# One projection of the second half computed before the attention instead of in between

## The chip, the cores and the metric

The kernel runs on one core of one Trainium2 chip. The metric is device time in microseconds (us) of one execution. TensorE (PE) does matrix products, VectorE (DVE), ScalarE (ACT) and GpSimd (POOL) do elementwise work, and SyncE (SP) issues nearly all DMAs, in the order of its own queue. Every engine takes its instructions in a fixed order and waits on semaphores.

## The reference, cut to what matters

A single decoder layer with 2048 tokens and a model width of 1024, all in float32:

```python
h = rmsnorm(x, g_norm)
proj = h @ w_in                       # 2048 x 1024 times 1024 x 9216
a_u, a_v, a_gate, q, k, v, b_gate, gate_logits = split(proj)
y_a = spatial_gating(gelu(a_u), gelu(a_v)) * silu(a_gate)
y_b = dilated_attention(q, k, v) * silu(b_gate)     # 16 heads, 3 patterns of keys
g_a, g_b = split(sigmoid(gate_logits))
merged = g_a * (y_a @ w_proj_a) + g_b * (y_b @ w_proj_b)
out = rmsnorm(x + merged @ w_out, g_final)
```

The change is about `b_gate`: columns 6144 to 7167 of `w_in`, called bg here, for the second half of the tokens (1024 of 2048). It is needed only where an attention output is multiplied by it.

## The kernel before, in words

**Precision.** Each float32 product is made of three products of split operands (hi times hi, hi times lo, lo times hi; `mm3`, L103). One output block of 128 channels by 512 tokens takes 8 slices of the inner dimension, so 24 matmuls of 128 by 512. The kernel's unit of work for bg is 16 such blocks per half (8 blocks of channels, 2 quarters of 512 tokens).

**Two ways to compute a projection.** `unit_T` computes the blocks one by one, 24 matmuls each, so 16 x 24 = 384 for bg of one half. It loads 128 columns of weights at a time (tile `wraw`), and GpSimd splits them into `whi` (L85) and `wlo` (L86). `unit_S` computes a 2 by 2 arrangement of blocks with seven block products in place of eight (Strassen's scheme in Winograd's form). It works with sums of weight blocks, which VectorE makes (L346 to L350), and sums of activation blocks (tiles `T`), which are made once per half. Each product has 12 matmuls, four groups of seven products make the same 16 blocks, so 336 matmuls. The price is more work elsewhere: ScalarE and GpSimd split the weights per product (L83, L86, tile `wc`), and VectorE adds the products together (L363).

**Stages.** For each half of the tokens: normalisation, v, the a_v projection, then k, q, and branch A (a_u and a_gate), nearly all with `unit_S`. In the first half two more `unit_S` follow: bg and the first gate (`ga`). In the second half the program goes from branch A to the attention after `restore`, which brings four activation tiles back (L150, L151, L144, L145) that had held sums. The results go to DRAM, bg to `bg_d`, from where the attention's last step loads them (L741).

**Attention and fill.** The function `window` writes out 16 heads, each with three patterns in the order p = 2, 1, 0, each with four groups g = 0 to 3. A group is in three stages: S (scores on PE, L639 and L640; bias, scale and row maximum on VectorE, L647; exponential on ScalarE, L653), T (transposes, L669; a split into `ph` on ScalarE, L672, and `pl` on VectorE, L673) and O (output products, L686 to L688; copy on ScalarE, L689). The stages are written in a software pipeline: S of group j, T of group j-2, O of group j-3. For each head come, in pieces between the stages, `combine` of the head before (VectorE L708 to L732, GpSimd L729, on every second head transposes L739 and L743) and `permuted`, which reorders Q, KH and KL (L600, L598) for the coming pattern.

Into this stream go the other products, the *fill*: block products of `unit_T`, cut into runs of 8 matmuls (`every` = 8). A run is put in when the fill counted so far lags behind the attention counted so far times a ratio. This ratio is the total fill, 5.2 us per block, less 8 blocks, over a nominal cost of the attention. Six blocks (144 matmuls) come before the first group, and what is left comes at the end. The stage `final` (the projection of the attention and the output) follows.

In this text heads are numbered 0 to 15, and "group p2 g0" means the stretch from the first output product (L686) of that group to the first of the next group. In this stretch PE does the O stage of this group, the S stage of the group three later, the T stage of the group one later, and whatever fill stands between.

## Time and profile before

| | |
|---|---|
| median of 3 runs (lowest to highest) | 2685.8 us (2683.05 to 2686.45) |
| the profiled execution: its time, its span | 2690.79 us, 2688.8 us |
| mean granted TensorE clock | 0.974 |
| busy: PE, DVE, ACT, POOL | 93%, 67%, 47%, 33% |
| attention's window (first fill matmul to the last output copy) | 1326.3 to 2281.4 us |
| of this, from the first output copy on | 1380.7 to 2281.4 us |

Where a row of the profile has the form `L103 PE MATMUL pj<-X,whi ... x1284 | 440.5, 416 | ...` it gives the line, engine, operation, tiles written and read, the number of instructions, their busy time in us and the mean duration of one in ns, and then the idle time before them. A row of stretches has begin and end, the length, and the busy time and number of instructions per engine, then the granted PE clock and the share and rate of the DMA engines. A PE that counts as busy isn't always at its peak, since the duration of a matmul reaches into the next one: in a dense stretch one of 128 by 512 starts every 0.23 us and lasts 0.39 us.

### The profile page before, as it was taken

Reading aid. Unit: us, or ns where it says so; the run is one execution under the profiler, and the core shown is the slowest. Engines: PE = TensorE matmul, PEld = TensorE weight load, DVE = VectorE, ACT = ScalarE, POOL = GpSimd, SP = SyncE. Lnnn points to the kernel's source line nnn. Section 1 sums busy time; section 2 is a strip of 40 time slices with the busy share of each in tenths; the row PEclk is TensorE's granted clock in tenths of the full one; section 3 lists DMA queues with packets and bytes.
Section 4 is the critical chain, followed back from the end, with each engine's and each line's share of the span. In section 5 each row is a group of like instructions: output and inputs, shape, how many; then the busy total and the mean of one; then the engine's idle time right before and its main releaser. Section 6 shows DMA issues by size and latency. Waiting matters only on the chain.

```text
span 2688.8 us, 45128 instructions
## 1 busy us (share of the span) xinstructions
PE 2503.2 (93%) x16736; PEld 2122.7 (79%) x16736; DVE 1794.8 (67%) x3633; ACT 1255.1 (47%) x2481; POOL 888.2 (33%) x633
## 2 busy tenths in 40 slices
PE   5969999999998999999899899989889898899998
PEld 5969888888887898888677778878777777677787
DVE  5864767756258547677457877787989888545533
ACT  4335333343333353333257777676767665222221
POOL 0325554444444444544222222333333333000000
PEclk9989999999999999999899999999999999999999
DMA  7744333253453343323356646677777876755541
GB/s 232 162 126 142 102 118 106 94 171 116 153 167 89 87 138 115 122 95 114 99 142 158 185 127 181 177 195 201 200 217 194 237 206 176 239 168 184 169 132 63
DMA packets 463995, 410.00 MB, mean 152 GB/s; under 512 B 150432, under 2 KB 384288, under 8 KB 463776
## 3 DMA queue, kind: packets, MB, share of 16 engines
q1 hardware_dynamic: 463344, 407.05, 51.7%
q8 instruction: 132, 2.16, 0.3%
q14 instruction: 87, 0.71, 0.1%
q10 hardware_dynamic: 432, 0.07, 0.0%
HBM read 297.35 MB, written 109.71 MB: 151 GB/s over the span
## 4 chain that ended last, share of the span: by engine, by line
PE 67%; DVE 13%; DMA 10%; issue 4%; ACT 3%; POOL 1%; SPq 0%; ACTq 0%; DVEq 0%; POOLq 0%
PE pj L103 32%; PE pt L103 15%; PE ss L103 10%; PE pt L669 3%; DVE S L647 2%; PE ss L639 2%; DVE pl L673 1%; DVE X L145 1%; PE ss L640 1%; DMA v_d<-vst 1%; DMA wraw<-in_w_in 1%; DMA OC<-o_d 1%; DMA o_d<-ob 1%; PE pt L512 1%; DVE OC L727 1%
## 5 line engine op out<-in xcount | busy, mean ns | idle before, releaser
L103 PE MATMUL pj<-X,whi 128*128 128x512 f32 x1792 | 602.3, 411 | 16.5 <-POOL whi L85 11.1
L86 POOL TENSOR_TENSOR wc<-wraw,wc 128x512 fp32r<-128x512 f32 x240 | 327.4, 1372 | 318.7 <-ACT wc L83 307.2
L103 PEld LDWEIGHTS pj<-X,whi 128*128 128x128 f32 x1792 | 342.5, 195 | 88.1 <-POOL whi L85 12.0
L103 PE MATMUL pj<-X,wlo 128*128 128x512 f32 x896 | 369.2, 412 | 7.6 <-DVE wlo L86 4.0
L647 DVE CUSTOM_DVE_ANT_0 S<-ss,B,niqk 128x256 f32<-128x256 f32 (+1 forms) x768 | 284.3, 418 | 22.0 <-PE ss L640 21.8
L673 DVE SCALAR_TENSOR_TENSOR pl<-pt,ph 128x512 f16<-128x512 f32 x320 | 204.8, 653 | 93.3 <-ACT ph L672 92.0
L653 ACT ACTIVATE S<-S,ob 128x128 f32<-128x128 f32 (+1 forms) x512 | 193.4, 437 | 72.5 <-DVE ob L647 71.5
L83 ACT CAST wc<-wraw 128x512 fp32r<-128x512 f32 x240 | 145.2, 618 | 165.3 <-PE pt L103 78.8
L85 POOL TENSOR_SCALAR whi<-wraw 128x1024 fp32r<-128x1024 f32 x64 | 69.9, 1093 | 442.9 <-PE pj L103 393.2
L103 PEld LDWEIGHTS pj<-X,wlo 128*128 128x128 f32 x896 | 175.1, 195 | 46.5 <-DVE wlo L86 6.9
L672 ACT ACTIVATE ph<-pt 128x512 f16<-128x512 f32 x320 | 177.2, 565 | 61.1 <-PE pt L669 37.0
L103 PE MATMUL ss<-T,wc 128*128 128x512 f32 x768 | 188.2, 394 | 0.0
L103 PE MATMUL pt<-X,wc 128*128 128x512 f32 x768 | 185.2, 390 | 0.0
L103 PE MATMUL pj<-WO,X 128*128 128x512 f32 x768 | 180.7, 395 | 4.1 <-ACT X L872 3.9
L103 PEld LDWEIGHTS pj<-WO,X 128*128 128x128 f32 x768 | 144.2, 188 | 40.0 <-ACT X L872 5.2
L669 PE MATMUL pt<-ident,S 128*128 128x128 f32 x1200 | 168.6, 278 | 3.4 <-DVE pl L673 3.3
L86 POOL TENSOR_TENSOR wcl<-wraw,wch 128x1024 fp32r<-128x1024 f32 x52 | 129.2, 2486 | 121.4 <-ACT wch L83 97.2
L103 PEld LDWEIGHTS ss<-T,wc 128*128 128x128 f32 x768 | 143.6, 188 | 32.0
L103 PEld LDWEIGHTS pt<-X,wc 128*128 128x128 f32 x768 | 143.9, 188 | 30.3
L86 POOL TENSOR_TENSOR wlo<-wraw,whi 128x1024 fp32r<-128x1024 f32 x64 | 164.5, 2571 | 5.3
L103 PE MATMUL pt<-T,wc 128*128 128x512 f32 x672 | 165.0, 394 | 0.0
L669 PEld LDWEIGHTS pt<-ident,S 128*128 128x128 f32 x1200 | 141.7, 144 | 15.1 <-DVE pl L673 4.4
(229 smaller groups left out, 5777.8 us busy)
## 6 DMA issues: line engine op xcount, KB each, us to landing
wraw<-in_w_in SPq DMA_DIRECT2D x64, 1024.0 KB, 5.7
V<-v_d SPq DMA_DIRECT2D x48, 520.0 KB, 4.8
o_d<-ob SPq DMA_DIRECT2D x32, 528.0 KB, 5.1
OC<-o_d SPq DMA_DIRECT2D x32, 528.0 KB, 4.7
wraw<-in_w_in SPq DMA_DIRECT2D x32, 512.0 KB, 5.4
wraw<-in_w_proj_a SPq DMA_DIRECT2D x32, 512.0 KB, 5.3
wraw<-in_w_proj_b SPq DMA_DIRECT2D x32, 512.0 KB, 4.7
xt<-in_xT SPq DMA_DIRECT2D x60, 256.0 KB, 4.3
```

The lines of the kernel that those rows point to most:

```text
L83: nc.scalar.copy(hi, raw)
L85: nc.gpsimd.tensor_scalar(out=hi, in0=raw, scalar1=1.0, scalar2=0.0, op0=ALU.mult, op1=ALU.add)
L86: self.w_lo.tensor_tensor(out=lo, in0=raw, in1=hi.bitcast(F32), op=ALU.subtract)
L103: self.pe = nc.tensor.matmul(out, st(a, k), mv(b, k), start=first and n == 0, stop=last and n == len(todo) - 1)
L145: self.x_lo.tensor_tensor(out=X[k][1], in0=src, in1=X[k][0].bitcast(F32), op=ALU.subtract)
L512: nc.tensor.matmul(px[:, i * P:(i + 1) * P], av[:, 4 * q + i], w, start=True, stop=True)
L639: nc.tensor.matmul(ps[:, i, :n], q, KH[:, w], start=True, stop=False)
L647: nc.vector.tensor_tensor_reduce(out=S[:, j, :n], in0=ps[:, i, :n], in1=B[:, bo:bo + n], scale=self.niqk[:, pr:pr + 1], scalar=3e38, op0=A ...
L653: nc.scalar.activation(S[:, i, :rng[i]], S[:, i, :rng[i]], AF.Exp, bias=ob[:, i, 65:66], scale=-1.0)
L669: self.pe = nc.tensor.transpose(px[:, j * P:(j + 1) * P], G["S"][:, i, c * P:(c + 1) * P], self.ident)
L672: nc.scalar.activation(ph[:, :n], px[:, :n], AF.Copy, scale=PSCALE)
L673: nc.vector.scalar_tensor_tensor(out=pl[:, :n], in0=px[:, :n], scalar=PSCALE, in1=ph[:, :n], op0=ALU.mult, op1=ALU.subtract)
```

## The change: what it does

bg of the second half is computed by `unit_S` right after branch A and ahead of `restore`, so before the attention. It no longer stands in the fill, whose total is given as 64 blocks instead of 80.

```diff
@@ Prog.run
                     drain(branch_a)
+                if hf == 1:
+                    drain(self.unit_S(X, win, 6144, self.ev_bg, qds))
                 if hf == 0:
                     drain(self.unit_S(X, win, 6144, self.ev_bg, qds))
                     drain(self.unit_S(X, win, 7168, self.ev_gate(self.ga_d), qds))
@@ fill()
             e = self.every
-            yield from self.unit_T(X, win, 6144, self.ev_bg, (2, 3), every=e)
             yield from self.unit_T(X, win, 7168, self.ev_gate(self.ga_d), (2, 3), every=e)
@@ 
-            self.window(at, fill(), 80 * 5.2)
+            self.window(at, fill(), 64 * 5.2)
```

How this moves instructions is seen on PE. First, the end of branch A. The last row that stays is a product of branch A (`wc` is a weight piece of `unit_S`); X and T are activations and their sums, `ss` a bank of PSUM.

```order
 L103 MATMUL pt<-T_3_1_6995,wc 128x512
 L103 MATMUL pt<-T_3_0_6994,wc 128x512
+L103 MATMUL ss<-X_0_0_6521,wc 128x512
+L103 MATMUL ss<-X_0_1_6522,wc 128x512
+L103 MATMUL ss<-X_0_0_6521,wc 128x512
+L103 MATMUL ss<-X_1_0_6523,wc 128x512
+L103 MATMUL ss<-X_1_1_6524,wc 128x512
```

In all 336 rows of this kind are new here, the 28 products of the unit; behind them the first row of the fill comes as before.

Second, PE in the attention, head 4, group p2 g0, from the last score product of the S stage on (`KLP` is the reordered low part of the keys). Before:

```order
L640 MATMUL ss<-KLP,Q 128x256
L103 MATMUL pj<-X_2_0_6525,wlo 128x512
L103 MATMUL pj<-X_3_0_6527,whi 128x512
L103 MATMUL pj<-X_3_1_6528,whi 128x512
L103 MATMUL pj<-X_3_0_6527,wlo 128x512
L103 MATMUL pj<-X_4_0_6529,whi 128x512
L103 MATMUL pj<-X_4_1_6530,whi 128x512
L103 MATMUL pj<-X_4_0_6529,wlo 128x512
L103 MATMUL pj<-X_5_0_6531,whi 128x512
L669 MATMUL pt<-ident,S 128x128 x4
L686 LDWEIGHTS ph
L686 MATMUL po<-V,ph 128x65
```

With the change, at the same place:

```order
L640 LDWEIGHTS Q
L640 MATMUL ss<-KLP,Q 128x256
L669 MATMUL pt<-ident,S 128x128 x4
L686 LDWEIGHTS ph
L686 MATMUL po<-V,ph 128x65
```

The one run of eight fill matmuls that this group had is gone, and the transposes follow the scores at once.

Third, PE in head 4, group p1 g2, from the last output product of the O stage on (`cb` is the combined output of two heads, whose transposes stand here). Before:

```order
L688 MATMUL po<-V,pl 128x65
L103 MATMUL pj<-X_2_0_6525,wlo 128x512
L103 MATMUL pj<-X_3_0_6527,whi 128x512
L103 MATMUL pj<-X_3_1_6528,whi 128x512
L103 MATMUL pj<-X_3_0_6527,wlo 128x512
L103 MATMUL pj<-X_4_0_6529,whi 128x512
L103 MATMUL pj<-X_4_1_6530,whi 128x512
L103 MATMUL pj<-X_4_0_6529,wlo 128x512
L103 MATMUL pj<-X_5_0_6531,whi 128x512
L739 MATMUL pt<-ident,cb 128x128 x4
L639 LDWEIGHTS Q
L639 MATMUL ss<-KH,Q 128x256
```

With the change:

```order
L688 MATMUL po<-V,pl 128x65
L739 MATMUL pt<-ident,cb 128x128 x4
L639 LDWEIGHTS Q
L639 MATMUL ss<-KH,Q 128x256
L640 LDWEIGHTS Q
```

Here one run of two is gone; the other, between the scores and the transposes, stays. Counted over all 192 groups in this way, 48 runs (384 matmuls) leave:

| group | from 2 runs to 1 | from 1 to 0 | from 0 to 1 |
|---|---|---|---|
| p2 g0 | | 15 | |
| p2 g1 to p1 g1 | 6 | 3 | 5 |
| p1 g2 and p1 g3 | 18 | | |
| p0 g0 to p0 g3 | 3 | 9 | 1 |

A head has 13 or 14 runs before (head 15 has 11) and 10 or 11 with the change (8). The six blocks ahead of the first group, the end of the fill, and the order of the attention's own work stay as they are.

## The prediction

> **What bounds the kernel now.** I read the busy shares first, then the stretches between the stages, then the attention group by group.
>
> ```profile
> PE 2503.2 (93%) x16736; PEld 2122.7 (79%) x16736; DVE 1794.8 (67%) x3633; ACT 1255.1 (47%) x2481; POOL 888.2 (33%) x633
> 560.13:637.27 77.14, 77.14 (x337) 63.07 (x336) 47.50 (x63) 35.38 (x63) 39.25 (x31) 1.00 0.53 174
> 1316.73:1326.31 9.58, 0.00 (x0) 0.00 (x0) 4.99 (x8) 1.43 (x3) 1.05 (x1) 0.62 0.83 238
> 1326.31:1380.70 54.39, 48.82 (x232) 38.10 (x232) 19.12 (x46) 20.68 (x28) 17.64 (x11) 0.91 0.65 174
> 1380.70:2281.40 900.70, 825.25 (x8080) 694.33 (x8080) 744.18 (x2228) 629.48 (x1389) 275.98 (x190) 0.97 0.68 187
> ```
>
> The line of the whole page says PE, 93% busy. But the average hides what matters here. The first stretch is bg of the first half, the very unit that the change writes a second time: PE is busy in all of it. The second is the idle time of PE between branch A and the first fill matmul, the third the six blocks of fill ahead, the fourth the attention. In the fourth PE idles 900.70 - 825.25 = 75 us, and VectorE is busy for 744 of 901 us (83%).
>
> Where is the idle time? Within a head there are two kinds of stretch. First the six groups from p2 g0 to p1 g1, for heads 1 to 14, each row from the first output product of the one to that of the other (14 rows and their sum):
>
> ```profile
> 1426.67:1456.26 29.59, 25.16 (x225) 21.09 (x223) 27.44 (x73) 22.46 (x47) 8.02 (x7) 0.94 0.45 126
> 1482.84:1511.28 28.44, 25.91 (x237) 21.54 (x234) 27.41 (x72) 22.27 (x47) 7.27 (x7) 1.00 0.51 146
> 1537.92:1567.97 30.05, 25.28 (x224) 21.25 (x222) 27.36 (x72) 22.81 (x48) 8.75 (x7) 0.89 0.40 115
> ...
> 2117.87:2148.22 30.35, 24.30 (x224) 19.59 (x224) 26.93 (x81) 21.63 (x45) 11.72 (x10) 1.00 0.84 227
> 2173.35:2202.89 29.54, 24.39 (x227) 20.31 (x227) 29.15 (x79) 20.24 (x43) 11.34 (x9) 1.00 0.53 145
> sum 417.48, PE 356.70 PEld 295.02 DVE 394.60 ACT 307.93 POOL 147.28; mean PE 25.48 PEld 21.07 DVE 28.19 ACT 21.99 POOL 10.52
> ```
>
> Here VectorE is busy for 394.60 of 417.48 us (95%) and PE idles 60.8. VectorE carries the combine of the head before and the reordering of the keys on top of the groups' own work. Then the six groups from p1 g2 to p0 g3:
>
> ```profile
> 1456.26:1482.84 26.58, 25.61 (x280) 21.85 (x278) 17.97 (x71) 18.41 (x43) 3.46 (x2) 1.00 0.67 168
> ...
> 2202.89:2232.00 29.11, 28.89 (x300) 24.60 (x298) 21.87 (x75) 17.30 (x46) 6.90 (x4) 1.00 0.83 252
> sum 387.85, PE 379.54 PEld 323.50 DVE 274.45 ACT 256.45 POOL 104.14; mean PE 27.11 PEld 23.11 DVE 19.60 ACT 18.32 POOL 7.44
> ```
>
> Here it is PE, 98% busy, with VectorE at 71%. So half of a head is bound by VectorE and half by PE, and a fill matmul taken away pays in the second half alone. The waits in the attention's window (total us, times, longest) say the same:
>
> ```profile
> PE ss L639 <- DVE ob L647: 38.7, 59, 4.3
> PE po L688 <- DVE pl L673: 18.4, 17, 3.0
> DVE S L647 <- PE ss L640: 21.8, 21, 4.6
> ```
>
> 57 us of PE's idle time are waits for VectorE, while VectorE waits for scores for 22 us.
>
> **What is added.** 28 products of 12 matmuls, with their weight splits, additions, tanh and 16 stores. The unit of the first half took 77.14 us, and PE was busy without a break while VectorE (47.50), ScalarE (35.38) and GpSimd (39.25) had room. The one of the second half has the same neighbours on one side (the order shows its first product right behind branch A's last); on the other it ends at `restore`, as branch A does now. Its weight loads replace loads of equal size in the fill, and SP has room for them. So I take +77.1 us, at 77.14 / 336 = 0.230 us per matmul. Since the unit was never held up, I see no reason for a range of more than a microsecond on this term.
>
> Does the start of the attention change? Its chain is this:
>
> ```profile
> 1319.56 0.75 DVE L151 SCALAR_TENSOR_TENSOR xt<-xt,gn,rsbc 128x512 f32<-128x512 f32 x1 [0.48 <-DMA xt<-in_xT]
> 1320.37 0.38 SPq L91 DMA_DIRECT2D wraw<-in_w_in  x1
> 1325.21 1.05 POOL L85 TENSOR_SCALAR whi<-wraw 128x1024 fp32r<-128x1024 f32 x1 [30.25 <-DMA wraw<-in_w_in]
> 1326.31 0.80 PE L103 MATMUL pj<-X,whi 128*128 128x512 f32 x1 [9.58 <-POOL whi L85]
> ```
>
> The first fill weights are loaded into memory that `restore`'s last multiplication (its `rsbc`) still holds, and PE waits 9.58 us. With the change `restore` stands behind bg, the same chain follows bg's last product, and in SP's order that load now comes just behind bg's last store instead of just ahead of branch A's. The evacuation has one VectorE operation less (0.69 us) per block. I take 0, between -1 and +1.
>
> **What is taken away.** 48 runs of eight fill matmuls, 384 matmuls, at most 384 x 0.230 = 88.2 us. By the table of the change 29 of them (net) leave the stretch bound by PE and 19 the one bound by VectorE.
>
> *From two runs to one, in the stretch bound by PE: 21.* The profile holds the experiment: p1 g2 and p1 g3 occur with two runs (17 times) and with one (11 times); these are the first row and the sum of each.
>
> ```profile
> 1456.26:1462.36 6.10, 6.10 (x54) 4.94 (x51) 4.15 (x12) 3.99 (x10) 0.00 (x0) 1.00 0.13 46
> sum 110.09, PE 109.20 PEld 90.29 DVE 72.33 ACT 66.89 POOL 13.75; mean PE 6.42 PEld 5.31 DVE 4.25 ACT 3.93 POOL 0.81
> 1511.28:1515.88 4.60, 4.60 (x49) 4.11 (x49) 2.92 (x11) 3.21 (x9) 0.74 (x1) 1.00 0.28 86
> sum 49.05, PE 48.82 PEld 42.23 DVE 40.66 ACT 33.32 POOL 23.41; mean PE 4.44 PEld 3.84 DVE 3.70 ACT 3.03 POOL 2.13
> ```
>
> 110.09 / 17 - 49.05 / 11 = 6.48 - 4.46 = 2.02 us per run. So -42.4 us; the lower bound is the bare matmuls, 21 x 1.84 = 38.6.
>
> *From one run to none, in the same stretch: 8 net, most in p0 g0.* In heads 1 to 14 no group there ran without fill. With one run:
>
> ```profile
> sum 45.98, PE 44.58 PEld 38.30 DVE 33.17 ACT 32.90 POOL 20.29; mean PE 4.05 PEld 3.48 DVE 3.02 ACT 2.99 POOL 1.84
> ```
>
> 11 of p0 g0, 4.18 us each, of which VectorE works 3.02 and ScalarE 2.99. Without the run PE needs 4.18 - 1.84 = 2.34, and VectorE becomes the bound at 3.02: 1.16 us are won, or up to 1.84 where the neighbours, in which VectorE has room, absorb it. I take the middle, 1.5: -12 us, between -9.3 and -14.7.
>
> *In the stretch bound by VectorE: 19 net, 15 of them the only run of p2 g0.* The sum of the 14 stretches of p2 g0, and ScalarE's reordering of Q, which stands in it:
>
> ```profile
> sum 63.65, PE 51.44 PEld 42.09 DVE 60.11 ACT 62.19 POOL 14.45; mean PE 3.67 PEld 3.01 DVE 4.29 ACT 4.44 POOL 1.03
> L600 ACT COPY QP<-Q x15: 4114/4162/4247, 1376.2 to 2171.2; 128x2048 f16<-128x2048 f16 x15
> ```
>
> ScalarE is busy for 62.19 of 63.65 us and VectorE for 60.11, so the 15 runs can win about 0.1 us each there, 1.5 in all. For the other four I take 1 us each, which makes -5.5 us. The bounds are 0 and all the time in which VectorE isn't busy in the six groups: (417.48 - 394.60) / 14 = 1.63 us per head, 26 us for 16.
>
> *bg's evacuation leaves the attention.*
>
> ```profile
> L544 DVE SCALAR_TENSOR_TENSOR tbg<-tbg,pj 128x512 f32<-128x512 f32 x16 | 11.0, 685 | 28.7 <-ACT tbg L543 23.8 <-DMA KH<-k_d 4.9
> L732 DVE TENSOR_TENSOR cb<-OC 128x256 f32<-128x256 f32 x64 | 43.0, 672 | 4.7 <-POOL OC L729 4.7
> L732 DVE TENSOR_TENSOR cb<-OC x60: 405/416/2623, 1436.0 to 2254.4; 128x256 f32<-128x256 f32 x60
> ```
>
> Sixteen of 0.685 us, ten of them among the groups, 6.9 us of VectorE; about half fall into the stretch it bounds: -3.5 us, between 0 and -6.9. The gate's evacuation (ScalarE alone) takes the places, so nothing new waits.
>
> The last two rows bear on a smaller thing. An L732 takes 0.416 us mostly, 0.672 in the mean. By the Trainium skill, page "GPSIMD Engine Reference", section "Specifications", GpSimd shares its memory interface with VectorE, and operations with two inputs from there are held up. The trace agrees in kind (405 to 2623 ns for one shape). By that rule eight weight splits fewer would win some 2 us more; I leave it out.
>
> The sum against the profiled execution (2690.8 us): +77.1 - 42.4 - 12 - 5.5 - 3.5 = **+13.7 us**, 2704.5. The median of the runs lies 5 us lower, and the change should read +13.7 there too: 2685.8 + 13.7, rounded to **2700 us**. With the bounds of the terms it is +30 (77.1 - 38.6 - 9.3 - 0 - 0 = 29.2, and 1 of the start) down to -13 (77.1 - 42.4 - 14.7 - 26 - 6.9).
>
> **The rivals.**
>
> *The slack of VectorE is used.* If PE's runs in the VectorE-bound groups cost time because PE comes late with scores, VectorE's 1.63 us per head would be won: 77.1 - 42.4 - 14.7 - 26 - 3.5 = -9.5, so 2676 us. For it: VectorE's 22 us of waits for scores. Against it: it is 95% busy, and in p2 g0 both VectorE and ScalarE are full. Half of that slack would be near no change.
>
> *The clock.* A p2 g0 without fill leaves PE idle longer: now (63.65 - 51.44) / 14 = 0.9 us, then 2.7. If PE gets half its clock for one more piece of 3.4 us per head, and half of it counts, 1.7 x 16 = 27 us are lost: +41, 2727 us. For it: the granted clock is under 1 in many of these stretches (0.94, 0.89). Against it: of the rows shown, those at 1.00 took 28.44, 29.54 and 30.35 us, and the one at 0.89 took 30.05, so VectorE hides it. It decides where PE's work at half clock outlasts VectorE's 28.2 us. The Trainium skill, page "TensorE: Matmul & The Clock Gate", section "Part 1", gives the piece as about 3.4 us, and says that one idle window throttles the array; the granted clock here agrees with pieces of that order, and no run here shows the threshold.
>
> *The start of the attention gets shorter.* If the first fill weights come while bg's last products run, the 9.58 us go, and the change is about +4: no change. Against it: the order above and `rsbc`.
>
> *The change doesn't shorten the attention at all*, since its own latency sets the pace: +77. Against it stand the 2.02 us per run, so I give it nothing of its own.
>
> **How the numbers follow.** Forecast 0.65, VectorE's slack used 0.13, the clock 0.14, the shorter start 0.08. Under 0.2% (5.4 us) this kernel's measurement doesn't tell a change. The forecast's own range is +3 to +28 (2689 to 2714), of which some 0.12 lie within 5.4 us. So faster 0.12 (nearly all of the slack's rival), the same 0.20 (0.12, and 0.08 of the shorter start), slower 0.68. The range from 2682 to 2722 reaches into the cases on both sides.
>
> **What would show it.** Right: the new unit shows some 77 us with PE busy throughout; p1 g2 to p0 g3 falls from 27.7 us (387.85 / 14) to about 24, with PE still over 95%; p2 g0 to p1 g1 stays at 29 to 30 us, with VectorE at 95% or more and PE's idle time grown from 4.3 us to over 5. Wrong: if p2 g0 to p1 g1 is shorter by over 1.5 us, runs paid there too; if it is longer than 31 us at a granted clock of 0.85, the clock decided; if the idle time ahead of the first fill matmul isn't 9 to 10 us, the start changed.

## The result and the profile after

| | before | with the change |
|---|---|---|
| median (lowest to highest, 4 runs each) | 2686.1 us (2683.1 to 2686.9) | 2716.3 us (2715.3 to 2717.5) |
| ratio, 95% interval | | 1.0115 (1.0097 to 1.0132) |
| span of the profiled execution | 2688.8 us | 2715.1 us |

The changed kernel is 30 us slower; +14 was forecast. Here are its stretches, in the columns of the rows in the prediction: the new unit (from its first matmul to the end of its last), PE's idle time ahead of the first fill matmul, the six blocks of fill ahead, the attention's groups, and the rest.

```profile
1311.97:1389.28 77.31, 77.31 (x337) 62.88 (x335) 41.08 (x59) 26.59 (x44) 28.07 (x21) 1.00 0.23 82
1389.28:1403.33 14.05, 0.00 (x1) 0.00 (x1) 3.88 (x6) 1.43 (x3) 1.05 (x1) 0.66 0.90 218
1403.33:1455.86 52.53, 45.89 (x224) 35.89 (x225) 15.81 (x47) 20.28 (x28) 18.97 (x11) 0.93 0.60 165
1455.86:2312.45 856.59, 750.76 (x7704) 634.02 (x7703) 734.56 (x2212) 617.05 (x1372) 251.52 (x174) 0.94 0.68 187
2312.45:2715.10 402.65, 380.21 (x1608) 302.38 (x1608) 187.02 (x278) 98.78 (x162) 15.87 (x22) 0.98 0.50 160
```

The last stretch of the kernel before was

```profile
2281.40:2688.80 407.40, 381.61 (x1608) 303.82 (x1608) 186.84 (x278) 98.73 (x162) 15.87 (x22) 0.98 0.50 158
```

So by stages: branch A ended at 1311.97 us instead of 1316.73 (-4.8); the new unit took **+77.3**; PE's idle time behind it grew from 9.58 to 14.05 us, **+4.5**; the fill ahead -1.9; the groups 900.70 became 856.59, **-44.1**; the rest -4.8, about as much as the profiled execution of before lay above its own median.

The first of these is scatter: nothing changed before the unit, and over all profiled executions of this document branch A's end lies at 1308.6 to 1316.7 us without the unit (8 executions) and at 1311.3 to 1318.3 with it (12). The idle time is not: it is 9.6 to 10.5 us in the 8 and 12.6 to 14.1 in the 12. PE waits there for the first fill weights (L91, `wraw`), and their load takes longer from issue to landing, last figure in the row, first before and then with the change:

```profile
wraw<-in_w_in SPq DMA_DIRECT2D x1, 512.0 KB, 4.6
wraw<-in_w_in SPq DMA_DIRECT2D x1, 512.0 KB, 9.4
```

So the added unit itself cost what was forecast, and the start of the attention 3.3 us in the mean of these executions, where nothing was expected. The groups should have given back 63.4 us and gave 44.1 in the profiled executions. (By the medians it is 77.3 + 3.3 - 30.2 = 50.4 us for all that follows, so 13 to 19 us are missing there.)

Where are these missing us? The forecast took a head as two stretches. Their sums over heads 1 to 14 with the change, p2 g0 to p1 g1 and p1 g2 to p0 g3, are

```profile
sum 415.79, PE 334.00 PEld 276.52 DVE 387.01 ACT 305.20 POOL 145.88; mean PE 23.86 PEld 19.75 DVE 27.64 ACT 21.80 POOL 10.42
sum 350.99, PE 335.50 PEld 288.49 DVE 277.64 ACT 248.31 POOL 88.17; mean PE 23.96 PEld 20.61 DVE 19.83 ACT 17.74 POOL 6.30
```

against 417.48 and 387.85 before. But this cut hides something: p0 g3, which belonged to the stretch bound by PE, has changed sides. So from here on a head is cut one group earlier. "The head's start" is p0 g3 to p1 g1 (seven groups), "the rest of the head" p1 g2 to p0 g2 (five). The sums over 14 heads, start and rest, before:

```profile
sum 468.15, PE 406.40 PEld 338.11 DVE 433.82 ACT 355.45 POOL 170.72; mean PE 29.03 PEld 24.15 DVE 30.99 ACT 25.39 POOL 12.19
sum 337.23, PE 329.89 PEld 280.59 DVE 235.50 ACT 209.74 POOL 80.70; mean PE 23.56 PEld 20.04 DVE 16.82 ACT 14.98 POOL 5.76
```

and with the change:

```profile
sum 476.83, PE 388.09 PEld 321.66 DVE 443.79 ACT 355.46 POOL 163.02; mean PE 27.72 PEld 22.98 DVE 31.70 ACT 25.39 POOL 11.64
sum 290.50, PE 281.74 PEld 243.64 DVE 221.35 ACT 198.05 POOL 71.44; mean PE 20.12 PEld 17.40 DVE 15.81 ACT 14.15 POOL 5.10
```

In these 14 heads 208 fill matmuls left the rest and 128 the start. The rest won 46.7 us, or 0.225 us per matmul: its full price. The start won nothing. It became **8.7 us longer** with 128 matmuls (28.8 us at the same price) less in it. These are sums over one execution each; a second execution of the same attention, in `e1_no_bg` below, has a start 4.1 us longer than before:

```profile
sum 472.28, PE 382.65 PEld 318.53 DVE 441.11 ACT 354.19 POOL 164.56; mean PE 27.33 PEld 22.75 DVE 31.51 ACT 25.30 POOL 11.75
```

VectorE is busy for 93% of it in both kernels, and its work there grew by 10.0 us, where 3.5 less had been expected.

PE's waits in the attention's window with the change (total us, times, longest):

```profile
PE po L686 <- ACT ob L689: 37.0, 14, 3.3
PE ss L639 <- DVE ob L647: 30.3, 41, 4.6
```

The first row was, before:

```profile
PE po L686 <- ACT ob L689: 11.3, 12, 1.4
```

Once per head PE now waits 2.6 us for ScalarE's copy of an output (L689), which stands behind the 4.2 us copy that reorders Q. The granted clock of the groups fell from 0.97 to 0.94. So there were several suspects: half clock after idle time, ScalarE's copy of Q, VectorE's load, and the place of the lost run itself.

### The profile page after: what moved, and what is told of

Its sections match the earlier page's. It is cut to its first block, busy times and chain, and to the rows that moved or that the text cites. A ratio compares the mean times of both kernels' runs of the same rounds, so it can differ in the third digit from the quotient of the medians.

```text
span 2715.1 us, 45188 instructions
## 1 busy us (share of the span) xinstructions
PE 2500.5 (92%) x16688; PEld 2120.7 (78%) x16688; DVE 1834.8 (68%) x3677; ACT 1270.2 (47%) x2513; POOL 901.2 (33%) x645
## 4 chain that ended last, share of the span: by engine, by line
PE 66%; DVE 14%; DMA 10%; issue 4%; ACT 4%; POOL 1%; SPq 1%; DVEq 0%; POOLq 0%; ACTq 0%
PE pj L103 31%; PE pt L103 16%; PE ss L103 11%; PE pt L669 2%; DVE S L647 2%; DVE pl L673 2%; PE ss L639 1%; DMA v_d<-vst 1%; DMA wraw<-in_w_in 1%; ACT S L653 1%; PE ss L640 1%; DVE X L145 1%; DMA wrow<-in_w_in 1%; PE pt L512 1%; DMA xl<-ya_d 1%
## 5 line engine op out<-in xcount | busy, mean ns | idle before, releaser
L103 PE MATMUL pj<-X,whi 128*128 128x512 f32 x1536 | 523.0, 417 | 20.9 <-POOL whi L85 14.8
L86 POOL TENSOR_TENSOR wc<-wraw,wc 128x512 fp32r<-128x512 f32 x264 | 358.9, 1367 | 358.1 <-ACT wc L83 339.9
L103 PEld LDWEIGHTS pj<-X,whi 128*128 128x128 f32 x1536 | 299.0, 198 | 85.1 <-POOL whi L85 15.7
L103 PE MATMUL pj<-X,wlo 128*128 128x512 f32 x768 | 318.5, 415 | 6.2 <-DVE wlo L86 3.3
L647 DVE CUSTOM_DVE_ANT_0 S<-ss,B,niqk 128x256 f32<-128x256 f32 (+1 forms) x768 | 284.1, 419 | 45.0 <-PE ss L640 44.7
L83 ACT CAST wc<-wraw 128x512 fp32r<-128x512 f32 x264 | 159.5, 617 | 179.2 <-PE pt L103 86.2
L103 PE MATMUL ss<-T,wc 128*128 128x512 f32 x816 | 200.1, 394 | 0.0
L103 PE MATMUL pt<-T,wc 128*128 128x512 f32 x768 | 188.4, 394 | 0.0
L103 PEld LDWEIGHTS pj<-X,wlo 128*128 128x128 f32 x768 | 151.0, 197 | 40.8 <-DVE wlo L86 6.2
L686 PE MATMUL po<-V,ph 128*128 128x65 f16 x1200 | 133.8, 194 | 39.9 <-ACT ob L689 37.0
L103 PEld LDWEIGHTS pt<-T,wc 128*128 128x128 f32 x768 | 144.0, 188 | 33.1
L86 POOL TENSOR_TENSOR wcl<-wraw,wch 128x1024 fp32r<-128x1024 f32 x52 | 129.1, 2484 | 119.8 <-ACT wch L83 93.6
```

The lines of the kernel that those rows point to most:

```text
L83: nc.scalar.copy(hi, raw)
L86: self.w_lo.tensor_tensor(out=lo, in0=raw, in1=hi.bitcast(F32), op=ALU.subtract)
L103: self.pe = nc.tensor.matmul(out, st(a, k), mv(b, k), start=first and n == 0, stop=last and n == len(todo) - 1)
L647: nc.vector.tensor_tensor_reduce(out=S[:, j, :n], in0=ps[:, i, :n], in1=B[:, bo:bo + n], scale=self.niqk[:, pr:pr + 1], scalar=3e38, op0=A ...
L686: nc.tensor.matmul(o, ph[:, sl], V[:, kb, 64:129], start=first, stop=False)
```

## The experiments

All ratios are to the kernel before as measured beside the run; its median lay between 2686 and 2691 us there. The changed kernel's own ratio is 1.0115.

### The unit alone

`e1_no_bg` leaves bg of the second half out of the changed kernel altogether; the attention's last step loads the first half's values.

```diff
-                if hf == 1:
-                    drain(self.unit_S(X, win, 6144, self.ev_bg, qds))
-            nc.sync.dma_start(out=sb, in_=self.bg_d[g][i * P:(i + 1) * P])
+            nc.sync.dma_start(out=sb, in_=self.bg_d[g % 2][i * P:(i + 1) * P])
```

> The changed kernel with the seven-product bg of the second half left out altogether (the attention's last step reads the bg of the first half in its place, so the work and the loads of that step stay). It measures the new unit and the gain of the window apart. All theories: the changed kernel's 2716 less the unit's 77 us, 2639 us, so 47 us below the kernel before. If the unit costs more than its own products (a longer start of the attention, or a delay carried into it), it is under 2635; if the window's gain was hidden by it, above 2643.

Measured: 2641.4 us, 0.9833 (0.9806 to 0.9861). The difference to the changed kernel, 1.0115 - 0.9833, is 76 us (67 to 85 by the intervals), and the window alone gives back 45 (37 to 52). Both sides of the balance are thus seen by themselves: the price of the unit with its longer start (77.3 + 3.3) lies within the first interval, and the gain in the attention is short of the 63.4 that were forecast.

### Half clock after idle time

`e2_dummy` and `e5_dummy2` put 16 transposes of the identity, which nobody reads, on PE ahead of one T stage per head, in place of the lost run (e5 with `G["g"] == 2`).

```diff
             px = self.pt()
+            if G["p"] == 2 and G["g"] == 1:
+                for _ in range(16):
+                    nc.tensor.transpose(px[:, :P], self.ident, self.ident)
```

> The changed kernel with 16 more transposes of the identity (0.11 us each, 1.75 us) per head ahead of the T stage of group p2 g1, so in p2 g0, where the run of fill went; they write over what the real transposes write over again and wait for nothing new. PE is as busy there as it was before. Clock theory (PE idles longer in p2 g0, its clock is halved for longer, and the work behind it is late; 24 us more of half clock among the groups): most of the missing 16 us come back, 2698 to 2704. VectorE theory (the stretch is bound by VectorE and ScalarE whatever PE does): 2713 to 2720. ScalarE theory (PE waits there for the copy of the output products behind the reordering of Q): 2713 to 2720, with the wait shorter by what the dummies take.

> As e2_dummy, but the 16 transposes stand ahead of the T stage of group p2 g2, which is where PE idles in p2 g0 (in e2_dummy they came a group earlier, in p0 g3, which they made 1.6 us longer). Clock theory: 2698 to 2704. ScalarE theory (PE waits 2.6 us per head there for the copy of the output products, the dummies take 1.75 of it): nothing changes, 2713 to 2719, and the wait for L689 falls from 37 to 10 or 15 us. VectorE theory: 2713 to 2719 too.

Measured: e2 2728.9 us, 1.0148 (1.0126 to 1.0169); e5 2725.0 us, 1.0140 (1.0108 to 1.0172). Neither won anything. In the stretch of a group stand the S stage of the group four later and the T stage of the group two later, not three and one as was said ahead of the prediction. So in e2 the transposes came to stand in p0 g3, where PE wasn't idle, and that group became 1.6 us longer per head; the run says little. In e5 they stand in p2 g0. These are the sums of p2 g0 and p2 g1 in the changed kernel:

```profile
sum 59.45, PE 25.90 PEld 23.69 DVE 53.74 ACT 57.71 POOL 37.80; mean PE 1.85 PEld 1.69 DVE 3.84 ACT 4.12 POOL 2.70
sum 89.22, PE 71.00 PEld 54.95 DVE 83.17 ACT 44.28 POOL 31.02; mean PE 5.07 PEld 3.93 DVE 5.94 ACT 3.16 POOL 2.22
```

and in e5:

```profile
sum 61.88, PE 50.23 PEld 48.22 DVE 54.69 ACT 58.26 POOL 39.19; mean PE 3.59 PEld 3.44 DVE 3.91 ACT 4.16 POOL 2.80
sum 83.30, PE 60.67 PEld 47.95 DVE 80.86 ACT 46.14 POOL 33.71; mean PE 4.33 PEld 3.42 DVE 5.78 ACT 3.30 POOL 2.41
```

The idle time of p2 g0 is filled (25.90 to 50.23 us of PE), and by the clock records the time lost to half clock in p2 g1 falls from 2.03 to 0.88 us per head, 16 us in all. The two groups together become 3.5 us shorter. So in these two groups half clock seems to be hidden behind VectorE for the most part. But the transposes also moved other work: p0 g3 grew by 10.4 us over the 14 heads, and over the whole starts the time lost to half clock fell only from 41 to 35 us. So the runs don't measure the clock by itself.

### ScalarE's copy of Q

`e3_no_qp` (changed kernel) and `e6_before_no_qp` (kernel before) drop the reordered Q of p2; the scores read Q in steps of 16 elements.

```diff
-            k[0] = self.permute(at, nc.scalar.copy, Q, "QP", p, 1).rearrange("p (b a) -> p b a", a=P)
+            k[0] = Q.rearrange("p (a q) -> p q a", q=16)
```

> The changed kernel without ScalarE's reordering of Q for pattern 2 (4.16 us per head); the score products read Q in steps instead, as those of pattern 1 do. The result is the same numbers. ScalarE theory (PE's 37 us of waits for L689 stand behind this copy): they go, 2680 to 2690. VectorE theory: p2 g0 is still held by VectorE (3.84 of 4.25 us busy), 2705 to 2716. Clock theory: PE idles less in p2 g0, so 2700 to 2708. If weight loads in steps of 16 elements were slow, 256 x 2 of them would show it on PE.

> The kernel before without ScalarE's reordering of Q, the control of e3_no_qp. Without that copy the changed kernel won about 20 us, 3 of them at the start of the attention. Cover theory (the run of fill in p2 g0 kept PE busy during the copy, the change took it away, and PE's wait for the copy is what the forecast missed): before wins the 3 us of the start and little else, 2676 to 2684 where before reads 2686, so the change costs 16 to 24 us without the copy. If the copy costs the same with and without the run: 2664 to 2670, and it explains nothing of the change.

Measured: e3 2699.8 us, 1.0041 (1.0028 to 1.0054); e6 2671.3 us, 0.9945 (0.9927 to 0.9964). In e3 the wait for L689 is gone from the profile, and another has grown by some 70% of it (30.3 to 56.7 us):

```profile
PE ss L639 <- DVE ob L647: 56.7, 42, 5.5
```

The scores read in steps hardly cost PE more. In e3 they share a row with those of p1 (the row of the kernel before is 219 ns, shown further below):

```profile
L639 PE MATMUL ss<-KHP,Q 128*128 128x128 f16 x320 | 56.3, 233 | 41.2 <-DVE ob L647 39.7
```

The copy costs 20 us in the changed kernel and 15 in the one before. It is a cost of both, and explains some 5 of the missing us (the intervals leave room for 8 more or less).

### VectorE's load

`e4_light` multiplies one of the three patterns by its weight in the combination instead of all three (the other two enter unscaled).

```diff
-                nc.vector.tensor_mul(OC[:, :, r, :HD], OC[:, :, r, :HD],
-                                     w[:, :, r, None].broadcast_to([P, 3, 4, HD]))
+                nc.vector.tensor_mul(OC[:, 0:1, r, :HD], OC[:, 0:1, r, :HD],
+                                     w[:, 0:1, r, None].broadcast_to([P, 1, 4, HD]))
```

> The changed kernel with the combine's large multiplication on VectorE (L727 before) done for one of the three patterns alone (the other two go unscaled into the sum), 64 instructions of about 0.4 instead of 1.06 us, 2.6 us per head less for VectorE in its own stretch. VectorE theory: nearly all of it shows, 35 to 42 us, 2675 to 2682. Clock and ScalarE theories: PE then idles less too, but its waits for ScalarE and the half clock stay, so 15 to 25 us, 2691 to 2701.

Measured: 2696.9 us, 1.0037 (1.0021 to 1.0054), 21 us less than the changed kernel. The rows of L727 in the changed kernel and in e4:

```profile
L727 DVE TENSOR_TENSOR OC<-OC,w 128x768 f32<-128x768 f32 x64 | 65.3, 1022 | 0.1
```

```profile
L727 DVE TENSOR_TENSOR OC<-OC,w 128x256 f32<-128x256 f32 x64 | 33.2, 521 | 0.1
```

32 us less of VectorE's work won 21, so two thirds of this work count. That is a bound of the kind that the forecast had named, but it was not run on the kernel before, so it doesn't say how the change altered it.

### One run given back

`e7_borrow` (changed kernel) and `e8_borrow_before` put one run of fill per head into p2 g0 out of turn and count it later, so that p0 g0 and p0 g1 have one less.

```diff
+            if 12 <= j < n and (j - 4) % 12 == 0:
+                self.seg(fill)
+            if 12 <= j < n and (j - 4) % 12 == 8:
+                state["fill"] += 0.217 * self.every
             if 2 <= j < n + 2:
```

> The changed kernel with one run of fill per head given back to p2 g0 (15 of 16 heads) and taken from p0 g0 or p0 g1 instead; the number of runs is the same. Cover theory: a run costs nothing in p2 g0 and pays its 1.84 us in p0: 22 to 29 us less, 2687 to 2694. VectorE theory (what PE wins in its own stretch VectorE gives back, since it enters the combine with more of its work left): 2704 to 2714. Clock theory: PE is warm in p2 g0: 2685 to 2692.

> The kernel before with the same borrowing: p2 g0 has two runs, p0 g0 one less. In p2 g0 PE idled 0.9 us per head before, with ScalarE at 98%. Cover theory: about half of a run fits, 16 x 0.9: 2668 to 2676 where before reads 2686. VectorE theory: 2682 to 2690.

Measured: e7 2689.4 us, 1.0007 (0.9988 to 1.0027); e8 2674.0 us, 0.9934 (0.9909 to 0.9959). Moving 15 runs won 29 us. The same move won 15 to 18 in the kernel before, so it undoes half of what the change had lost; the other half it would have won anyway. Start and rest of the 14 heads in e7:

```profile
sum 465.78, PE 395.45 PEld 329.06 DVE 443.04 ACT 362.84 POOL 168.49; mean PE 28.25 PEld 23.50 DVE 31.65 ACT 25.92 POOL 12.04
sum 273.30, PE 260.07 PEld 226.26 DVE 225.04 ACT 194.01 POOL 67.12; mean PE 18.58 PEld 16.16 DVE 16.07 ACT 13.86 POOL 4.79
```

Against the changed kernel the start has 112 matmuls more and is 11.1 us **shorter**, while VectorE does the same there (443.04 against 443.79). The rest, 112 matmuls poorer, is 17.2 us shorter. That reads as if the run's absence had cost something at the start. But e7's profiled execution was 7 us under its median, and the median alone allows the milder reading that the run costs nothing there: 15 runs taken from p0 at 1.80 us are 27 us, and 29 were won. The 2689 us lie in what was expected by the cover theory and by the clock theory alike, so the run doesn't part them; it does speak against the VectorE theory (2704 to 2714). And the move changed more than one place: VectorE's copy KHP for the next head, which started in p0 g3 in 9 of heads 1 to 14 with the change, starts there in one, and half clock at the starts fell from 41 to 15 us.

### The key copies moved away

`e9_late_keys` (changed) and `e10_late_keys_before` hold back VectorE's two key copies for the next head's p2 (L600) until after the score reductions of p0 g0.

```diff
+        late = lambda: self.tc.issue_after(self.red.ins) if p == 2 and hasattr(self, "red") else nullcontext()
+        with late():
-        k.append(self.permute(at, nc.vector.tensor_copy, KH, "KHP", p, 2))
+            k.append(self.permute(at, nc.vector.tensor_copy, KH, "KHP", p, 2))
...
+        if p == 0 and g == 0:
+            self.red = red
```

> The changed kernel with one thing added: VectorE's two copies that reorder the keys for the next head's p2 (L600, KHP and KLP, about 4.2 us per head) may not be issued before the score reductions of p0 g0, that is they leave the stretch that VectorE bounds and stand where it has room. Theory one (VectorE's fixed list of work bounds p0 g3 to p1 g1, so that runs of fill taken out there win nothing): most of the copies still in that stretch, some 2 to 3 us per head, is won, so 30 to 45 us of the changed kernel's excess of 1.0115: a ratio to before of 0.995 to 1.000. Theory two (PE's own chain of scores, transposes and products per group sets the pace there, VectorE only follows): no gain, 1.010 to 1.013. Theory three (half clock after idle PE): the same as theory two or a little better, 1.005 to 1.012.

> The same constraint in the kernel before. Theory one: the copies stand in the bound stretch in nearly every head here, so up to 4.2 us per head, limited by PE, which is busy for 25.5 of 29.8 us: 40 us or so, a ratio of 0.983 to 0.988. With VectorE out of the way a run of fill is worth its full price in both kernels, so e9 less e10 should shrink from +30 us to between +13 and -5. Theory two: 0.997 to 1.003, and e9 less e10 stays at +30.

Measured: e9 2718.4 us, 1.0101 (1.0081 to 1.0120); e10 2668.0 us, 0.9916 (0.9894 to 0.9937). The kernel before won 22 us, the changed one nothing, and the difference between the two grew to 50 us instead of shrinking. The first theory had it the other way round. Start and rest in e10:

```profile
sum 438.66, PE 394.90 PEld 329.20 DVE 403.51 ACT 335.15 POOL 175.69; mean PE 28.21 PEld 23.51 DVE 28.82 ACT 23.94 POOL 12.55
sum 349.14, PE 335.37 PEld 283.94 DVE 272.38 ACT 232.65 POOL 85.83; mean PE 23.95 PEld 20.28 DVE 19.46 ACT 16.62 POOL 6.13
```

and in e9:

```profile
sum 457.12, PE 383.74 PEld 319.30 DVE 417.12 ACT 333.10 POOL 150.82; mean PE 27.41 PEld 22.81 DVE 29.79 ACT 23.79 POOL 10.77
sum 311.36, PE 292.01 PEld 248.58 DVE 261.87 ACT 221.46 POOL 72.40; mean PE 20.86 PEld 17.76 DVE 18.70 ACT 15.82 POOL 5.17
```

In both kernels the start lost its copies: 30 us of VectorE in e10, 27 in e9. The start became 29.5 us shorter in e10 and 19.7 in e9. The rest took the copies in, and grew by 11.9 in e10 but by 20.9 in e9. PE's idle time there grew by 6.4 us in e10 and by 10.6 in e9, which has a run less in p1 g2 and p1 g3 behind which the copies could be hidden. So e9's gain at the start was paid back, all of it, in the rest. Both profiled executions lie within 1.4 us of their medians, and between them the start is 18.5 us longer with 128 matmuls less: the clearest sign that taking fill out of a start can cost time.

### All three cures together

`e11_best_before` and `e12_best_after`: late key copies, no copy of Q, one run given back.

> Kernel before with three things: the late key copies, no reordering of Q for p2 by ScalarE (the scores read Q in steps of 16), and one run of fill per head moved from p0 to p2 g0. The last two gave -15 and -17 us alone. If the three add up: 0.970 to 0.975; if they all cure the same idle time: as the best of them, 0.985.

> The changed kernel with the same three. If the runs of fill left out of the window are now all worth their price, it is at or below e11 (77 added, up to 88 taken away): 0.967 to 0.975. If the stretch from p0 g3 to p1 g1 is still bound by something other than PE, it stays 10 to 30 us above e11.

Measured: e11 2664.3 us, 0.9903 (0.9874 to 0.9932); e12 2685.1 us, 0.9985 (0.9969 to 1.0000). They don't add up (-26 us, where -22, -15 and -18 had been seen alone), so they cure in part the same idle time, or meet the next bound. e11 is faster than both kernels; e10, with one of the three, can't be told from it. The change still costs 21 us on top.

### No reordering copies at all

`e13_no_copies` (changed) and `e14_no_copies_before`: the scores of p1 and p2 read Q and the keys where they lie.

```diff
-        k.append(self.permute(at, nc.vector.tensor_copy, KH, "KHP", p, 2))
+        q = 16 if p == 2 else 4
+        k.append(KH.rearrange("p (a q) -> p q a", q=q))
         yield
-        k.append(self.permute(at, nc.vector.tensor_copy if p == 2 else nc.scalar.copy, KL, "KLP", p, 2))
+        k.append(KL.rearrange("p (a q) -> p q a", q=q))
```

`e15_no_copies_borrow` and `e16_no_copies_borrow_before` give one run per head back on top.

> The changed kernel without any reordering copy: the scores of p1 and p2 read Q and the keys where they lie, in steps of 4 and 16 elements. Per head VectorE loses 5.8 us (2.2 + 2.1 + 1.5) and ScalarE 6.2 (4.1 + 2.1). Theory one (VectorE's whole load: 47.5 us per head against 47.8 of PE, and no room to move it to): most of PE's 7.0 idle us per head go, 60 to 80 us in all, 2635 to 2655, a ratio to before of 0.980 to 0.990. Theory two (the chain of scores, transposes and products with its short buffers sets the pace; of VectorE and ScalarE only the copy of Q matters): -20 us as without the copy of Q, 1.003 to 1.005. If the keys read in steps cost PE time, both this kernel and e14 are longer by it.

> The kernel before without any reordering copy. PE idles 4.9 us per head here. Theory one: 40 to 60 us won, a ratio of 0.978 to 0.985, and e13 less e14 comes out between -11 and +8 us, since with VectorE out of the way each run left out is worth its 1.8 us. Theory two: 15 us won as without the copy of Q, 0.993 to 0.996, and e13 less e14 stays near +30.

> e13 with one run of fill per head moved from p0 to p2 g0. Theory one: little on top of e13, 0 to -10 us, since p2 g0 is then no longer held by ScalarE and VectorE. Theory two: -29 us as in the changed kernel.

> e14 with one run of fill per head moved from p0 to p2 g0. Theory one: within 8 us of e14. Theory two: -15 us, as in the kernel before.

Measured: e13 2747.8 us, 1.0224 (1.0207 to 1.0241); e14 2731.3 us, 1.0162 (1.0147 to 1.0178); e15 2733.6 us, 1.0172 (1.0149 to 1.0195); e16 2722.1 us, 1.0130 (1.0115 to 1.0145). All are slower, since the keys read in steps cost PE time. The scores with 128 columns in the kernel before (p2's alone) and in e13, where 256 of the 336 are p2's, in steps of 16, 64 are p1's, in steps of 4, and 16 are p0's, in no steps:

```profile
L639 PE MATMUL ss<-KHP,QP 128*128 128x128 f16 x256 | 36.3, 219 | 3.9 <-DVE ob L647 2.3 <-DVE OC L647 1.4
```

```profile
L642 PE MATMUL ss<-KH,Q 128*128 128x128 f16 x336 | 129.7, 386 | 14.6 <-DVE ob L650 14.1 <-DVE OC L650 0.3
```

With that, PE has more to do and VectorE less, and PE bounds nearly everywhere. The starts of the 14 heads in e14 and e13:

```profile
sum 446.70, PE 442.26 PEld 344.56 DVE 369.09 ACT 283.80 POOL 158.63; mean PE 31.59 PEld 24.61 DVE 26.36 ACT 20.27 POOL 11.33
```

```profile
sum 442.51, PE 422.76 PEld 328.70 DVE 380.33 ACT 283.15 POOL 141.24; mean PE 30.20 PEld 23.48 DVE 27.17 ACT 20.23 POOL 10.09
```

e13 less e14 is +16 us and e15 less e16 +12. The change costs 14 to 18 us less than between the two kernels themselves, though not the -11 of full price that theory one would give at its best. That would fit if what PE and VectorE have to do relative to each other decides part of it. The levels of both theories were wrong by the price of the steps, which the expectations had named without a size.

### A second run

`e17_borrow2` puts two runs per head into p2 g0 and p2 g1, taken from p1 g3 to p0 g1; `e18_borrow2_no_qp` does the same without the copy of Q.

```diff
+            if 12 <= j < n and (j - 4) % 12 in (0, 1):
+                self.seg(fill)
+            if 12 <= j < n and (j - 4) % 12 in (7, 8):
+                state["fill"] += 0.217 * self.every
```

> The changed kernel with two runs of fill per head moved from p1 g3 to p0 g1 into p2 g0 and p2 g1, so that p0 g3 to p2 g2 has 39.4 fill matmuls per head and p1 g2 to p0 g2 has 20.6 in place of 36.6. Theory one (at a head's start fill costs nothing up to some 39 matmuls, since VectorE, ScalarE and the hand-overs among them set the time there): the start stays at 18.8 to 19.8 us, p1 g2 to p0 g2 falls from 20.75 to 17.2 to 17.8 us, 2665 to 2680 in all, a ratio to before of 0.990 to 0.998. Theory two (a run costs its 1.8 us there as well once the idle time of p2 g0 is filled): the start grows by 1.7 us over one run given back, nothing is won over it, 0.999 to 1.003.

> The same without ScalarE's reordering of Q for p2. Theory one: the start, 18.33 us with 24 fill matmuls without that copy, grows to 18.8 to 19.5 with 39.4, and p1 g2 to p0 g2 is as short as in the run beside it: 2655 to 2672, a ratio of 0.987 to 0.994, below both kernels. Theory two: 0.997 to 1.003.

Measured: e17 2706.9 us, 1.0077 (1.0053 to 1.0102); e18 2701.6 us, 1.0046 (1.0029 to 1.0063). Both theories missed. From p0 g3 to p2 g2 the time was as flat as theory one had it: 19.26 us per head with 40 matmuls, 18.78 with 32 in e7. But one group further, in p2 g3, the sum of 14 heads went from 69.34 us in e7 to

```profile
sum 107.90, PE 74.36 PEld 57.10 DVE 105.28 ACT 70.46 POOL 37.36; mean PE 5.31 PEld 4.08 DVE 7.52 ACT 5.03 POOL 2.67
```

VectorE is busy for 105 of 108 us in it. The stall of a head's start hadn't gone; it had moved on, together with VectorE's pile of work. PE's idle time of 2.3 to 2.4 us stood in p2 g1 before the change, in p2 g0 with it, and in p2 g3 in e17.

### The pairs side by side

Seven pairs of kernels differ by the change alone (e1, e2, e4, e5, e17 and e18 have no partner). In each, 128 matmuls leave the starts of the 14 heads and 208 the rests; the differences are those of sums as above.

| pair (with less before) | starts, us | rests, us | fill in p2 g0 | difference of the medians, us | half clock at the starts, us |
|---|---|---|---|---|---|
| the two kernels | +8.7 | -46.7 | 8 to 0.6 | +30 | +15 |
| without the copy of Q (e3, e6) | +0.7 | -41.1 | 8 to 0.6 | +28 | +19 |
| late key copies (e9, e10) | +18.5 | -37.8 | 8 to 0.6 | +50 | +23 |
| no copies (e13, e14) | -4.2 | -41.2 | 8 to 0.6 | +16 | +10 |
| one run given back (e7, e8) | -15.0 | -35.4 | 16 to 8.6 | +15 | 0 |
| all three (e12, e11) | -15.9 | -36.4 | 16 to 8.6 | +21 | +5 |
| no copies, one given back (e15, e16) | -12.0 | -47.1 | 16 to 8.6 | +12 | +9 |

The last column is the difference of the time lost to half clock: the length of the starts times what the granted clock lacks to 1, summed over the heads. All columns but that of the medians are from one execution of each kernel, which lies up to 8 us from its median.

The rests always win 35 to 47 us. The starts go with the place of the run: where p2 g0 keeps one they win 12 to 16 us, where its only run goes they win 4 or lose up to 19. The means of the two groups (-14.3 and +5.9) are 20 us apart, about the size of what was missing. But within the second of these groups alone the spread is 23 us, and the pairs that differ by the given run alone are less clear: 24 us for the two kernels, 8 us without copies, and by the medians 15 and some 5. The last column goes with the starts just as well: half clock grows by 10 to 23 us where the only run goes, by 0 to 9 where one stays. So the pairs don't tell whether the run, the half clock behind a longer idle PE, or both set the difference.

## Why the prediction was right or wrong

**Right: the unit.** +77.1 forecast, +77.3 measured; the 76 by e1 hold the start of the attention too.

**Wrong, by a little: the start of the attention.** The step is "I take 0, between -1 and +1". PE's idle time went from 9.58 to 14.05 us, and from 10.1 to 13.4, so by 3.3 us, in the mean of all profiled executions. The chain is the one that the forecast named, but the load in it takes 9.4 us instead of 4.6. Why was not varied; the forecast had seen that the load moves behind bg's last store, and gave that no price. The shorter start falls as a rival: the start grew.

**Right, but a little high: the runs in the stretch bound by PE.** The rests of the heads gave 0.225 us per matmul, 1.80 per run. The forecast took 2.02 for the 21 runs that leave one behind, from groups that differ in more than the run, and 1.5 for the other eight, so 1.88 in the mean. Over 26 runs in 14 heads the 0.08 make some 2 us.

**Wrong: the head's start.** The step that failed is "In the stretch bound by VectorE: 19 net", -5.5, with "bg's evacuation leaves the attention", -3.5. The two said that the stretch keeps its bound and gets 9 us shorter. Cut as the prediction cut it, p2 g0 to p1 g1 became 1.7 us shorter, and p0 g3, which the forecast held in the stretch bound by PE and from which no run was taken, 9.9 us longer (387.85 - 337.23 = 50.62, then 350.99 - 290.50 = 60.49). Some 6 of the 9.9 us stand in one head, whose p0 g3 took 10.31 us where the others took 3.49 to 4.97. The forecast's reading "VectorE and ScalarE are full, so the run of p2 g0 wins about 0.1" asked only what the run's absence could win, and put a floor of zero under it. What the runs showed in its place is a start that gets longer: by 4 to 9 us in the two executions with the change, by 18.5 with late key copies. The pairs go with the last run of p2 g0, as if it had stood between PE and a stall; that it was this run is argued, not shown.

Two things in the trace show what the floor had left out. First, it was taken that the attention's own work keeps its order, since PE's rows did. VectorE's did not. Its copy KHP for the next head (L600) stood in p0 g3 in 3 of heads 1 to 14 before, and in 9 with the change. Score reductions (L647) move from the rest into the start as well. These are the sums of the 14 stretches of p0 g3 that open the starts, all work and then L647 alone, before:

```profile
sum 50.67, PE 49.70 PEld 43.09 DVE 39.22 ACT 47.53 POOL 23.44; mean PE 3.55 PEld 3.08 DVE 2.80 ACT 3.39 POOL 1.67
sum 50.67, DVE 17.96; mean DVE 1.28
```

and with the change:

```profile
sum 61.04, PE 54.09 PEld 45.14 DVE 56.78 ACT 50.26 POOL 17.15; mean PE 3.86 PEld 3.22 DVE 4.06 ACT 3.59 POOL 1.22
sum 61.04, DVE 31.69; mean DVE 2.26
```

So VectorE enters the start with more work left, 13.7 us of it score reductions, and fills p0 g3 to 93% where it had filled 77%: what PE wins in the rest, VectorE gives back in part behind it. Second, GpSimd's weight splits come at other moments. VectorE's small operations of the combination (L713, L717, L718) in the kernel before:

```profile
L713 DVE TENSOR_TENSOR lw<-w,OC x16: 236/248/1466, 1425.2 to 2281.8; 128x48 f32<-128x48 f32 x16
L717 DVE TENSOR_SCALAR mn<-mn,ihv x16: 217/228/690, 1430.2 to 2282.8; 128x16 f32<-128x16 f32 x16
L718 DVE TENSOR_TENSOR w<-w,mn x16: 187/208/2012, 1431.5 to 2283.0; 128x48 f32<-128x48 f32 x16
```

and with the change:

```profile
L713 DVE TENSOR_TENSOR lw<-w,OC x16: 231/247/700, 1496.9 to 2312.9; 128x48 f32<-128x48 f32 x16
L717 DVE TENSOR_SCALAR mn<-mn,ihv x16: 216/235/2334, 1500.7 to 2313.9; 128x16 f32<-128x16 f32 x16
L718 DVE TENSOR_TENSOR w<-w,mn x16: 194/210/2292, 1503.0 to 2314.1; 128x48 f32<-128x48 f32 x16
```

The three lines cost 19 us of VectorE in the window before and 27 after. But they are the ones that stand at the start. All nine small operations (L708 to L718) cost 49 us before and 51 after, since the first three, which stand in the rest, got 6 us cheaper: the delay moved into the start rather than grew. Neither of the two was varied alone. e9 took the copies out of the start and won nothing in all, since the rest lost what the start won, so no run shows that their place is the cause.

**The rivals.** "The clock" gave the nearest time (2727 us, measured 2716), and the granted clock did fall as it said, 0.97 to 0.94 over the groups. In e5 16 us less half clock in p2 g1 came with 3.5 us less time in p2 g0 and p2 g1, which speaks against it as the main cause; but over the starts e5 took away only 6 of the 41 us, and the pairs' starts go with the half clock as well as with the run. It stays a rival for a part of the missing us, perhaps a large one. That its time came nearest doesn't count for it: it left out the longer start of the attention. "VectorE's slack is used" falls: the starts got longer, not shorter. "The change doesn't shorten the attention at all" falls with the 44 us.

**The signs named.** The unit at 77 us came true. The idle time ahead of the first fill matmul was to stay at 9 to 10 us, or the start had changed: it is 14.05, so it had. p1 g2 to p0 g3 was to fall to about 24 us with PE over 95%: it is 25.1 with 95.6% (350.99 / 14; 335.50 of 350.99), most of the excess being in p0 g3. p2 g0 to p1 g1 stayed at 29.7 us and PE's idle time rose to 5.8, as said, but VectorE is at 93%, not 95.

**What stays open** is whether it is the last run of p2 g0 that matters, and why: order on VectorE and ScalarE, the moment of GpSimd's splits, and the clock all change with it, and no run here changed one of them alone. Also open is why the first fill weights land later behind bg.

## What to carry to other kernels

A stretch that another engine bounds doesn't make fill worthless there. Taking it away can make the stretch longer, so "it wins nothing to take it away" needs a lower bound below zero. When a change takes work out of an instruction stream that a scheduler orders, compare the order of every engine near the bound, not of the engine that the change touches. And place what is left: moving one run per head won 29 us here, and 15 to 18 in the kernel before, too. Last, the price of a new stage can include the wait behind it: here the next stage's first load landed later, and PE waited 3 to 4 us longer.

## What the runs showed of the hardware

- VectorE operations of 0.2 us on 128x16 and 128x48 elements took up to 2.33 us. With the change seven of them took over 2 us, and all seven overlap GpSimd's two-input weight split (L86). In four cases the split took 4.0 us then, in the other three its usual 2.3:

```profile
L86 POOL TENSOR_TENSOR wlo<-wraw,whi x56: 2343/2390/4022, 1403.4 to 2323.1; 128x1024 fp32r<-128x1024 f32 x56
```

  The Trainium skill, page "GPSIMD Engine Reference", section "Specifications", has the shared memory interface of the two; the trace agrees, and shows that both sides can lose.
- A load of 512 KB took 4.6 us from issue to landing ahead of the attention in the kernel before and 9.4 with the change (4.6 to 5.5 and 7.6 to 9.4 over all executions). No run varied what stood ahead of it.
- Reading the stationary operand of a float16 product in steps of 16 elements cost next to nothing (rows of 219 and 233 ns per product, the second with p1's 64 products in it; without the copy the kernels were 20 and 15 us faster). Where the moving one was read in steps too, the row shows 386 ns in place of 219, of 256 products in steps of 16, 64 in steps of 4 and 16 in none.
